# One run of products per piece of the paged cache: scores of piece u beside values of piece u-1

## The chip, the cores and the metric

The kernel runs on one core of a Trainium2 chip. The metric is the device time of one execution in microseconds, as the median over timed runs. The core has a matrix engine (TensorE, PE in the profile; its weight loads are PEld), a vector engine (DVE), a scalar engine (ACT), GpSimd (POOL), a queue engine (SP), and 16 DMA engines that all queues share.

## What is computed

One decoder layer for a prompt group of 512 tokens and a sample group of 8 sequences with 8 tokens each. The 576 tokens are normed and pass one input projection (1024 to 5632 columns). Its columns feed a differential attention (4 heads, two softmax maps each), a gated linear recurrence (4 heads) and two gates. The branches are merged, projected and added to the residual; then come a mixture of 16 experts (two per token), a per-layer input and a last norm.

The change is in the attention of the sample group alone. Its 8 sequences each look at 4096 earlier tokens, which lie in 32 pages of 128 tokens in a paged cache of keys and values. Cut to that part, the reference says:

```python
def page_step(carry, pages):                    # carry: maximum, sum, weighted values
    kp = cache_k[layer, pages]
    vp = cache_v[layer, pages]
    s = jnp.einsum('bthcd,bshcd->bhcts', q, kp).astype(jnp.float32) * scale
    return _online_softmax_update(carry, s, vp), None
carry, _ = lax.scan(page_step, (m0, l0, a0), page_table.T)
```

So for each sequence, head, map and token: scores against all cached keys, their softmax, and the weights times the cached values. All of it is kept in 32-bit floats.

## The kernel before

The kernel's Python builds the whole program ahead of time. Each strand of the work is a "lane", a generator that issues instructions and yields where it needs an event, a free buffer, or nothing but a turn. `run_lanes` picks at each step, among the lanes that can go on and whose estimated time has been reached, the one with the lowest priority number. The estimates come from cost functions (`_cost_pe` and others, and 350 GB/s plus 2 us for a DMA); a DMA's event carries its estimated landing. They count nothing for a change between kinds of product (`SWITCH = 0.0`). The order in which the lanes issue is the order in which each engine runs; on the chip the engines wait only for semaphores, and TensorE goes through its products in that order.

The paged cache is worked off in 32 pieces: a piece u is 8 pages of one sequence, four pieces to a sequence. A piece has four gathers of keys and four of values. Each gather is an indirect DMA of 128 rows of 4 KB (512 KB), issued from GpSimd by `lane_kv`. The order there is four gathers of keys first, then keys and values in turn, so that the keys are always four gathers (one piece) ahead of the values. The buffers are few: NK = 3 tiles for keys that hold two gathers each, and NV = 5 for values that hold one each. GpSimd takes its issues in order, so a gather that waits for a free buffer holds up those behind it.

`lane_scores` makes a piece's scores in two halves, each as soon as its two gathers of keys are in (`kev`), then takes the maximum (DVE), the exponentials (ACT), turns the weights round with four transposes (TensorE) and copies them to `ptz` (two of them); event `ptev[u]`. `lane_values` waits for `ptev[u]`, and for each of the piece's four gathers of values (`vev`) before the products with it. Between the second and the third it yields a turn:

```python
                if j % VW == VW - 1:
                    self.free("V")
                if j == 1:
                    yield
```

Both kinds of product use 32 columns of stationary operand, four heads side by side in the array (`128*32` in the profile). As 32-bit products they show as two instructions each: 32 instructions with 256 moving columns for the scores of a piece, 64 with 128 columns for its values. Most other products use all 128 columns (`128*128`), those of the input projection (`in<-H,hi` and `in<-H,lo`, 288 columns) above all. These belong to `lane_main`, which has a higher priority number and so fills what the other lanes leave. Beside them run the prompt's attention, the recurrence and the routing.

`lane_batches` finishes a sequence after its fourth piece. When all of these lanes and the input projection are through, `lane_mid` closes their buffers; the second branch, the output projection and the experts follow.

Of the kernel before, what the change touches and what calls it, by code (L numbers as in the profile page):

```python
# [20 lines left out]
NB = 8  # L21
# [10 lines left out]
EPS = 1e-6  # L32
# [10 lines left out]
def _consts():  # L43
    """Tables that depend on the shapes alone."""
    p = np.arange(128)
# [54 lines left out]
VW = 1  # L100
# [38 lines left out]
# the weights' chunks in the order of their use  # L139
# [17 lines left out]
def _horder():  # L157
    """The halves of the experts' weights in the order of their use: an expert's second product runs beside the next one's first."""
    r = []
    for tl in range(NE + 2):  # L160
        k, b = wkey(tl), wkey(tl - 1)
        now = [(*k, q) for q in range(4)] if tl <= NE else []
        then = [(*b, q) for q in (4, 5)] if tl else []
        r += now[:2] + then[:1] + now[2:] + then[1:]
    return r + [("pg", k) for k in range(8)]
# [19 lines left out]
class Engine:  # L185
    """Passes instructions on and keeps an estimate of the engine's clock, by which the lanes are interleaved."""
# [62 lines left out]
class Kern:  # L249
# [16 lines left out]
    # ------------------------------------------------ lanes  # L266
# [39 lines left out]
    def pick(self, *tags, n=1):  # L306
        """Which of several tags has n slots free: one that ends in o is for the further tiles until they are through."""
        def f():
            for t in tags:
                if (t[-1] == "o" if self.inner else t[-1] != "o" or self.fev.t is not None):  # L310
                    if self.used.get(t, 0) + n <= self.cap.get(t, 0) - (0 if self.gapev.t is None else self.mres if t == "mr" else self.hres if t == "H" else 0):
                        return t
            return None
        return f
# [12 lines left out]
    def pool(self, st, name, tags, **kw):  # L327
        """A pool with a number of slots per tag, counted as the lanes take and free them."""
# [26 lines left out]
    def aside(self, f):  # L355
        """Runs f without making the lane wait for what it issues; returns the time it ends."""
# [9 lines left out]
    def rstd(self, ss, n, shape):  # L366
        """(ss / n + EPS) ** -0.5 by Newton's steps from the exponent's estimate."""
# [23 lines left out]
    # ---------------------------------------------------------------- start  # L391
# [19 lines left out]
    def setup_rest(self):  # L411
        nc, a = self.nc, self.a
        # lambda, on every partition
# [12 lines left out]
        # 1 for the first map's rows, -lambda for the second's  # L426
# [5 lines left out]
        # lower bound of the forget gate: f = fa + fb * tanh(z / 2)  # L432
# [22 lines left out]
    def lane_start(self):  # L455
        """x * g_mix in two parts, and the norm's factor per token along the free dimension."""
# [87 lines left out]
    # ---------------------------------------------------------------- input projection  # L544
    def issue_w(self, j):
        """Half j % 2 of chunk j // 2 of the weights."""
# [38 lines left out]
    def in_proj(self, i):  # L585
        """One tile of 128 columns of the input projection, for all tokens, with the norm's factor."""
# [68 lines left out]
    def lane_gates(self):  # L655
        """The branches' gates, back from memory."""
# [12 lines left out]
    def to_tok(self, z, tok, tail):  # L669
        """[128, 576] to the token-major [128, 4, 128] and [64, 128]."""  # L670
# [11 lines left out]
    def rope(self, x, c0, c1, sh):  # L682
        """Rotates x ([128, ...] with the positions c0..c1 last) in place."""
# [58 lines left out]
    def lane_attn(self):  # L742
        """Scores and weights of the prompt's attention, by head and block of queries."""
# [38 lines left out]
    def lane_mid(self, waits, st):  # L782
        """When the first phase's lanes are through, their space goes to the next phase's inputs."""
# [13 lines left out]
    # ------------------------------------------------ sample: the new tokens  # L797
# [35 lines left out]
    # ------------------------------------------------ sample: the paged cache  # L833
# [18 lines left out]
    def lane_scores(self):  # L852
        """Scores of 8 pages at a time by (head, page of a pair, token, map), their maxima, weights and sums."""
# [7 lines left out]
        nc.gpsimd.memset(self.xm, 0.0)  # L861
        yield self.qev
        self.query(0)
        for u in range(4 * NB):
            b, q = u // 4, u % 4
            if q == 0 and b > 2:
                yield self.finev[b - 3]
            if q == 2 and b + 1 < NB:
                self.query(b + 1)
            qbd = self.qbd[b].rearrange("p x a n -> p x (a n)")  # L870
            yield ("sc", 1)
            sc = self.tl("sc", [128, 4, 128])
            for j in range(2):
                yield self.kev[4 * u + 2 * j + 1]
                ks = self.ks[2 * u + j].rearrange("p j (d h n) -> p d h j n", d=2, h=4)
                for dh in range(2):
                    for h in range(4):
                        nc.tensor.matmul(sc[32 * h:32 * h + 32, 2 * j:2 * j + 2], qbd[:, h * 2 + dh], ks[:, dh, h], start=dh == 0, stop=dh == 1)
                self.free("K")
# [19 lines left out]
            self.set(self.ptev[u])  # L899

    def lane_values(self):
        nc = self.nc
        acc = self.tl("acc", [128, 4, 128])
        nc.raw.vector.memset(acc, 0.0)
        self.ob = []
        for u in range(4 * NB):
            b, q = u // 4, u % 4
            yield self.ptev[u]
            pt = self.ptz[u % 2].rearrange("p v y h a n -> p v y h (a n)")
            for j in range(4):  # L910
                yield self.vev[4 * u + j]
                vs = self.vs_[(4 * u + j) // VW][:, j % VW].rearrange("p (y h e) -> p y h e", y=2, h=4)
                for y in range(2):
                    for h in range(4):
                        nc.tensor.matmul(acc[32 * h:32 * h + 32, q], pt[:, j % 2, 2 * y + j // 2, h], vs[:, y, h],
                                         start=j == 0 and y == 0, stop=j == 3 and y == 1)
                if j % VW == VW - 1:
                    self.free("V")
                if j == 1:
                    yield  # L920
            self.used["pt"] -= 1
            if q == 3:
                yield ("ob", 1)
                ob = self.tl("ob", [128, 4, 128])
                nc.scalar.copy(ob, acc)
                self.ob.append(ob)
                self.set(self.accev[b])
        self.free("acc")
# [76 lines left out]
    # ------------------------------------------------ prompt attention  # L1005

    # ------------------------------------------------ gated linear recurrence
# [10 lines left out]
    # ---------------------------------------------------------------- branches, output projection  # L1018
# [57 lines left out]
    def rows_setup(self):  # L1076
        """Constants and weights of the routing."""
# [31 lines left out]
    def lane_route(self, i):  # L1109
        """The router's logits of a tile of tokens; its rows with the norm's weights, and behind them what belongs to the norm itself."""  # L1110
# [56 lines left out]
    # ---------------------------------------------------------------- routing  # L1167
# [3 lines left out]
    # ---------------------------------------------------------------- experts  # L1171
# [16 lines left out]
    def lane_msplit(self, keys):  # L1188
        """The first tiles' weights, while the routing is under way."""
# [4 lines left out]
    def lane_mx(self, tiles):  # L1194
        """The tokens' rows of each tile."""
# [26 lines left out]
    # ---------------------------------------------------------------- per-layer input, end  # L1222


    # ---------------------------------------------------------------- all of it
    def run(self):
# [21 lines left out]
        with ExitStack() as ctx:  # L1248
# [18 lines left out]
                     (self.lane_wsplit(), 0), (self.lane_zero(), 0), (self.lane_scores(), 1), (self.lane_values(), 1),  # L1267
# [22 lines left out]
    def more(self, n, who=None):  # L1290
        """A wait for n slots of F beyond those that the other lanes are sure of."""
        return ("F", lambda: n + sum(v for k, v in self.sure.items() if k != who))

    def lane_pv(self):
        """Weights times values, and each head's norm."""
# [49 lines left out]
    def lane_hprep(self):  # L1345
        """Gates, decays and the token-major parts of each head of the recurrence."""
# [51 lines left out]
    def lane_hblocks(self):  # L1398
        """The recurrence's chunks, its norm and its gate."""
        nc = self.nc  # L1400
        for h in range(4):
# [44 lines left out]
            # the sample group: one chunk of 8 per sequence, from its state  # L1446
# [35 lines left out]
            # norm over v, output gate  # L1482
# [36 lines left out]
    def lane_dispatch(self):  # L1519
        """Each token's two experts; token of each slot of each tile, row of each token's two results, experts of the further tiles."""  # L1520
# [129 lines left out]
        # the two weights: softmax over the pair, times the group's probability  # L1650
# [17 lines left out]
    def mload(self, key):  # L1668
        """A half of one part of the experts' weights, 512 KB."""
# [18 lines left out]
    def lane_tail(self, moe):  # L1688
        """Adds each token's experts, then the per-layer input behind its gate and the last norm, tile after tile."""
# [88 lines left out]
        def mixed(gens, rest):  # L1778
            """Steps of chains of small operations, with larger ones between them."""
# [44 lines left out]
    def further(self):  # L1824
        """Tiles beyond the first further one, where the data calls for them."""
# [14 lines left out]
    def query(self, b):  # L1840
        """A batch's queries, apart by page and map: column (page, token, map) of each head and half."""
# [7 lines left out]
    def lane_zero(self):  # L1849
        """The rows of further tiles that stay unused hold zeros."""  # L1850
# [362 lines left out]
```

## Time and profile before

| what | us | share of the span |
|---|---|---|
| median of 3 timed runs (1030.49 to 1032.61) | 1030.66 | |
| span of the profiled execution, first to last instruction | 1028.9 | |
| TensorE busy with products | 957.8 | 93% |
| TensorE's weight loads, beside them | 766.8 | 75% |
| DVE busy | 675.4 | 66% |
| ACT busy | 433.4 | 42% |
| POOL busy | 344.0 | 33% |
| products `sc<-K,qbd` (scores of the cache), 1024 instructions | 68.9 | |
| products `acc<-V,ptz` (values of the cache), 2048 instructions | 80.8 | |

The span is the profiled execution's own time without what lies around its first and last instruction; the timed runs include that. Busy time of TensorE is no measure of how full it is, since its products overlap; the distance between starts is what one more product costs. All records of the program carry the line of one helper (L209), so the groups are told apart by the tiles that they write and read.

### The profile page before, as it was taken

The numbers are of one execution on the slowest core, as the hardware profiler recorded it, in microseconds if no ns is written. First come the engines' busy times: TensorE is split into PE (matmuls) and PEld (weight loads), VectorE is DVE, ScalarE is ACT, GpSimd is POOL, SyncE is SP. The second block draws the span as 40 slices with busy tenths as digits, with TensorE's granted clock in tenths as the row PEclk, the third lists the DMA queues.
The fourth block names the chain that finished last, engine by engine and source line by source line (L and its number), as shares of the span: only waits on it lengthen the run. The fifth ranks groups of instructions, "written<-read, shape, count | busy, mean of one in ns | idle before, by whom it ended". The sixth has DMA issues, their size and how long they took to land. (4 is left out here: it accounts for less than half of the span.)

```text
span 1028.9 us, 20982 instructions
## 1 busy us (share of the span) xinstructions
PE 957.8 (93%) x8129; PEld 766.8 (75%) x8129; DVE 675.4 (66%) x1701; ACT 433.4 (42%) x875; POOL 344.0 (33%) x370
## 2 busy tenths in 40 slices
PE   6999999999999999999999989989639999998995
PEld 5986787877877878778878879868427777775683
DVE  6554555567866774864764465433778999996775
ACT  5143544353342323123222232232228888886442
POOL 3125545454455453543463111332340110101200
PEclk9999999999999999999999989999869999998998
DMA  7549989998989898897997437854149999993511
GB/s 235 206 154 406 367 304 341 313 299 287 335 306 344 311 333 284 297 348 240 332 342 289 139 106 264 291 195 179 46 158 326 393 413 411 412 413 136 186 42 51
DMA packets 93066, 278.67 MB, mean 271 GB/s; under 512 B 10288, under 2 KB 15168, under 8 KB 92960
## 3 DMA queue, kind: packets, MB, share of 16 engines
q0 software_dynamic: 42880, 155.28, 42.5%
q1 hardware_dynamic: 48496, 118.73, 31.7%
q10 hardware_dynamic: 1584, 3.24, 0.8%
q8 instruction: 67, 1.10, 0.4%
q14 instruction: 39, 0.32, 0.1%
HBM read 251.95 MB, written 25.27 MB: 269 GB/s over the span
## 5 line engine op out<-in xcount | busy, mean ns | idle before, releaser
L209 PE MATMUL in<-H,hi 128*128 128x288 f32 x1592 | 357.0, 315 | 14.1 <-ACT hi L209 5.9
L209 PEld LDWEIGHTS in<-H,hi 128*128 128x128 f32 x1592 | 258.9, 193 | 52.1 <-issue 31.3
L209 PE MATMUL in<-H,lo 128*128 128x288 f32 x796 | 239.1, 300 | 0.5 <-DVE lo L209 0.5
L209 POOL DMA_INDIRECT V<-in_vc,idxv x128 | 127.8, 998 | 192.1 <-PE acc L209 172.7
L209 POOL DMA_INDIRECT K<-in_kc,idxk x128 | 126.4, 987 | 104.9 <-PE sc L209 58.1
L209 PEld LDWEIGHTS in<-H,lo 128*128 128x128 f32 x796 | 153.2, 193 | 1.5 <-DVE lo L209 1.2
L209 PE MATMUL in<-mw,xs 128*128 128x512 f32 (+1 forms) x462 | 119.3, 405 | 0.0
L209 DVE TENSOR_TENSOR lo<-raw,hi 128x512 fp32r<-128x512 f32 x116 | 79.7, 691 | 49.5 <-ACT hi L209 48.2
L209 ACT CAST hi<-raw 128x512 fp32r<-128x512 f32 x116 | 70.1, 616 | 84.8 <-PE in L209 58.7
L209 PEld LDWEIGHTS in<-mw,xs 128*128 128x128 f32 (+1 forms) x462 | 85.3, 190 | 20.2 <-DVE xs L209 0.3
L209 PE MATMUL acc<-V,ptz 128*32 128x128 f32 x2048 | 80.8, 277 | 2.1 <-DMA V<-in_vc,idxv 2.0
L209 ACT COPY F<-aux 128x512 f32<-128x512 f32 (+3 forms) x74 | 30.0, 405 | 115.5 <-PE aux L209 115.4
L209 DVE TENSOR_TENSOR mw<-mr,mw 128x1024 fp32r<-128x1024 f32 x58 | 69.2, 1220 | 3.4 <-ACT mw L209 3.4
L209 PEld LDWEIGHTS acc<-V,ptz 128*32 128x32 f32 x2048 | 51.8, 109 | 24.0 <-issue 16.0
L209 PE MATMUL sc<-K,qbd 128*32 128x256 f32 x1024 | 68.9, 387 | 0.7 <-DMA K<-in_kc,idxk 0.7
L209 ACT CAST mw<-mr 128x1024 fp32r<-128x1024 f32 x63 | 65.0, 1056 | 9.0 <-DMA hf_d<-F 7.1
L209 POOL DMA_INDIRECT X<-hf_d,slots x16 | 15.4, 964 | 109.7 <-DVE mw L209 106.0
L209 PE MATMUL aux<-F,F 128*128 128x128 f32 (+6 forms) x216 | 48.0, 394 | 0.2 <-ACT F L209 0.2
L209 DVE TENSOR_TENSOR F<-in,rb 128x288 f32<-128x288 f32 x62 | 27.9, 451 | 29.7 <-PE in L209 29.5
L209 PEld LDWEIGHTS sc<-K,qbd 128*32 128x32 f32 x1024 | 28.3, 110 | 24.0 <-issue 9.3
L209 ACT ACTIVATE F<-F 128x576 f32<-128x576 f32 (+1 forms) x33 | 22.4, 680 | 51.1 <-POOL F L209 26.4
L209 PE MATMUL aux<-mw,hs 128*128 128x512 f32 x150 | 41.8, 415 | 0.5 <-ACT hs L209 0.5
(399 smaller groups left out, 1549.6 us busy)
## 6 DMA issues: line engine op xcount, KB each, us to landing
mr<-in_w_gu SPq DMA_DIRECT2D x55, 512.0 KB, 8.6
raw<-in_w_in SPq DMA_DIRECT2D x88, 256.0 KB, 5.0
mr<-in_w_dn SPq DMA_DIRECT2D x22, 512.0 KB, 10.4
y_d<-Yo SPq DMA_DIRECT2D x17, 512.0 KB, 11.4
raw<-in_w_br SPq DMA_DIRECT2D x16, 256.0 KB, 2.9
raw<-in_w_out SPq DMA_DIRECT2D x16, 256.0 KB, 5.8
H<-in_w_gu SPq DMA_DIRECT2D x7, 512.0 KB, 8.7
y_d<-G SPq DMA_DIRECT2D x1, 3584.0 KB
```

What stands on the lines that cost most here:

```text
L209: return f(*a, **kw)
```

## The change

The lane of the values is gone. The lane of the scores goes through 33 turns instead of 32 pieces. In turn u it waits for everything that the turn needs: the last gather of keys of piece u, the last gather of values of piece u-1, and the weights of piece u-1 (before: each half of the scores waited for its own two gathers, each quarter of the values for its own). Then it issues the scores of u and the values of u-1 with no yield between them, and frees the buffers. The first turn has scores alone, the last one values alone. The rest of a piece (maximum, exponentials, transposes, copies), the buffers, the gathers and their order are as before. Besides, comments and docstrings are gone.

```diff
-        for u in range(4 * NB):
+        for u in range(4 * NB + 1):
             b, q = u // 4, u % 4
+            new = u < 4 * NB
+            if new:
...
+                yield ("sc", 1)
+                sc = self.tl("sc", [128, 4, 128])
+                yield self.kev[4 * u + 3]
+            if u:
+                yield self.vev[4 * u - 1]
+                yield self.ptev[u - 1]
+                if u % 4 == 0:
+                    yield ("ob", 1)
+            if new:
...
+                for j in range(2):
+                    ks = self.ks[2 * u + j].rearrange("p j (d h n) -> p d h j n", d=2, h=4)
+                    for dh in range(2):
+                        for h in range(4):
+                            nc.tensor.matmul(sc[32 * h:32 * h + 32, 2 * j:2 * j + 2], qbd[:, h * 2 + dh], ks[:, dh, h], start=dh == 0, stop=dh == 1)
+                    self.free("K")
+            if u:
+                self.aside(lambda: self.values(u - 1, acc))
+            if not new:
+                break
             yield
...
-    def lane_values(self):
+    def values(self, u, acc):
...
-            for j in range(4):
-                yield self.vev[4 * u + j]
...
-                if j == 1:
-                    yield
...
-                     (self.lane_wsplit(), 0), (self.lane_zero(), 0), (self.lane_scores(), 1), (self.lane_values(), 1),
+                     (self.lane_wsplit(), 0), (self.lane_zero(), 0), (self.lane_scores(), 1), 
```

The body of `values` is the loop of the old lane without its yields: four gathers, for each eight products, then `free("V")`; after a sequence's fourth piece the copy of `acc` to `ob`.

## Rows read from the trace of the kernel before

**Rows 1.** Windows by stage: length, busy time (instructions) per engine, PEclk, DMA share, GB/s
```profile
67.00:588.00 521.00, 513.26 (x5827) 407.14 (x5829) 320.00 (x950) 174.96 (x454) 251.59 (x258) 1.00 0.88 311
588.00:625.00 37.00, 33.67 (x233) 30.82 (x226) 24.03 (x71) 13.06 (x30) 3.76 (x7) 0.86 0.38 110
625.00:763.00 138.00, 111.60 (x632) 90.12 (x630) 74.14 (x213) 36.31 (x70) 44.06 (x36) 0.93 0.54 190
763.00:925.00 162.00, 153.29 (x725) 121.87 (x726) 147.15 (x172) 135.55 (x187) 19.76 (x33) 0.98 0.99 385
```

**Rows 2.** Waits: who waited for whom, us in total, times, longest
```profile
POOL V L209 <- PE acc L209: 172.7, 80, 8.2
...
POOL K L209 <- PE sc L209: 58.1, 23, 28.8
...
PE acc L209 <- DMA V<-in_vc,idxv: 2.0, 1, 2.0
...
PE sc L209 <- DMA K<-in_kc,idxk: 0.7, 1, 0.7
```

**Rows 3.** Timeline of TensorE, a quarter of values, half of scores: start, length, instruction
```profile
572.56 0.43 PE L209 MATMUL in<-H,hi 128*128 128x288 f32 x2
...
573.05 0.65 PE L209 MATMUL acc<-V,ptz 128*32 128x128 f32 x16
573.62 0.54 PE L209 MATMUL in<-H,hi 128*128 128x288 f32 x2
...
574.13 0.43 PE L209 MATMUL in<-H,hi 128*128 128x288 f32 x2
...
574.53 0.43 PE L209 MATMUL in<-H,hi 128*128 128x288 f32 x2
...
575.01 1.07 PE L209 MATMUL sc<-K,qbd 128*32 128x256 f32 x16
576.01 0.53 PE L209 MATMUL in<-H,hi 128*128 128x288 f32 x2
...
576.52 0.43 PE L209 MATMUL in<-H,hi 128*128 128x288 f32 x2
```

**Rows 4.** Timeline of TensorE, a stretch that holds both kinds
```profile
512.43 0.43 PE L209 MATMUL in<-H,hi 128*128 128x288 f32 x2
...
512.92 1.07 PE L209 MATMUL sc<-K,qbd 128*32 128x256 f32 x16
513.80 1.06 PE L209 MATMUL acc<-V,ptz 128*32 128x128 f32 x32
514.79 0.54 PE L209 MATMUL in<-H,hi 128*128 128x288 f32 x2
...
515.30 0.43 PE L209 MATMUL in<-H,hi 128*128 128x288 f32 x2
```

**Rows 5.** Timeline of TensorE, the cache's first and last stretch of products
```profile
67.14 1.93 PE L209 MATMUL sc<-K,qbd 128*32 128x256 f32 x32
...
587.84 0.65 PE L209 MATMUL acc<-V,ptz 128*32 128x128 f32 x16
```

**Rows 6.** Timelines of TensorE and POOL where gathers follow freed buffers
```profile
482.45 0.64 PE L209 MATMUL acc<-V,ptz 128*32 128x128 f32 x16
...
483.40 0.93 POOL L209 DMA_INDIRECT V<-in_vc,idxv  x1 [8.22 <-PE acc L209]
484.64 0.94 POOL L209 DMA_INDIRECT K<-in_kc,idxk  x1 [0.30 <-PE acc L209]
...
488.37 0.94 POOL L209 DMA_INDIRECT V<-in_vc,idxv  x1 [0.30 <-issue]
```

**Rows 7.** Instructions on tile V: from a gather's issue to its landing
```profile
DMA to landing us min/median/max: 4.0/6.7/9.7
```

**Rows 8.** Timeline of TensorE and ACT, from the last values to the sample's attention output
```profile
588.55 0.58 ACT L209 COPY ob<-acc 128x512 f32<-128x512 f32 x1 [0.51 <-PE acc L209]
...
608.36 0.30 PE L209 MATMUL aux<-constb,yo 128*128 128x128 f32 x1
```

More of the change, by code (lines that the diff above doesn't have):

```diff
@@ L861, in lane_scores @@
         nc.gpsimd.memset(self.xm, 0.0)
+        acc = self.tl("acc", [128, 4, 128])
+        nc.raw.vector.memset(acc, 0.0)
+        self.ob = []
         yield self.qev
         self.query(0)
-        for u in range(4 * NB):
+        for u in range(4 * NB + 1):
             b, q = u // 4, u % 4
[L866 to L879, printed above, removed]
+            new = u < 4 * NB
+            if new:
+                if q == 0 and b > 2:
+                    yield self.finev[b - 3]
+                if q == 2 and b + 1 < NB:
+                    self.query(b + 1)
+                yield ("sc", 1)
[7 more added lines that the diff above has]
+            if new:
+                qbd = self.qbd[b].rearrange("p x a n -> p x (a n)")
+                for j in range(2):
[8 more added lines that the diff above has]
+                break
             yield
@@ L899, in lane_scores @@
             self.set(self.ptev[u])
-    def lane_values(self):
+        self.free("acc")
+    def values(self, u, acc):
         nc = self.nc
[L903 to L909, printed above, removed]
-            for j in range(4):
-                yield self.vev[4 * u + j]
[L912 to L918, printed above, removed]
-                if j == 1:
-                    yield
[L921 to L928, printed above, removed]
+        b, q = u // 4, u % 4
+        pt = self.ptz[u % 2].rearrange("p v y h a n -> p v y h (a n)")
+        for j in range(4):
+            vs = self.vs_[(4 * u + j) // VW][:, j % VW].rearrange("p (y h e) -> p y h e", y=2, h=4)
+            for y in range(2):
+                for h in range(4):
+                    nc.tensor.matmul(acc[32 * h:32 * h + 32, q], pt[:, j % 2, 2 * y + j // 2, h], vs[:, y, h],
+                                     start=j == 0 and y == 0, stop=j == 3 and y == 1)
+            if j % VW == VW - 1:
+                self.free("V")
+        self.used["pt"] -= 1
+        if q == 3:
+            ob = self.tl("ob", [128, 4, 128])
+            nc.scalar.copy(ob, acc)
+            self.ob.append(ob)
+            self.set(self.accev[b])
     def lane_batches(self):
```

## The prediction

> **What bounds the kernel now.** I read the windows by stage first. From 67 to 588 us, where the cache is worked off, TensorE is busy for 513.26 of 521 us at the full granted clock, while DVE has 320 and POOL 252; the DMA engines stand at a share of 0.88 and 311 GB/s [rows 1]. The reader is to see an engine with no holes and a DMA that is heavily used but not full: in the experts' stage the same share reads 0.99 at 385 GB/s. Second come the waits, to see which of the two, TensorE or DMA, is behind the other. GpSimd's gathers wait for buffers that TensorE frees, 172.7 us for values and 58.1 for keys; TensorE waits for gathers 2.0 and 0.7 us [rows 2]. So the gathers run ahead, and TensorE's order sets the end of this stage. Third, the timeline of TensorE tells what a stretch of the cache's products costs.
>
> After 588 us nothing hangs on absolute time: the stage behind it is fed by products of the first, and in 625 to 763 the DMA share is 0.54, which leaves room for the experts' weights that are fetched early there [rows 1]. What the first stage gains, the end gains.
>
> **The price of a stretch.** Two starts of the `hi` pair of the input projection lie 0.40 us apart where nothing comes between (574.13 to 574.53). Over a quarter of values it is 572.56 to 574.13 for two such turns, so 1.57 - 0.80 = 0.77 us for 16 instructions; over half the scores 574.53 to 576.52, 1.99 - 0.80 = 1.19 us [rows 3]. A stretch that holds half the scores and two quarters of values costs 512.43 to 515.30, 2.87 - 0.80 = 2.07 us [rows 4]. Apart these three would be 1.19 + 2 x 0.77 = 2.73. The difference, 0.66 us, is two changes into the 32-column products and out again: **0.33 us for each stretch**, whatever its length. What is left is 0.86 us for half the scores and 0.44 for a quarter of values.
>
> The part of the rows that shows it: the first `hi` pair behind a stretch lasts 0.53 to 0.54 instead of 0.43 us, and its next one starts 0.51 later instead of 0.40 [rows 3]. The Trainium skill (TensorEngine Tiling (Array Packing), Key Properties) says that changing the tiling mode drains the engine, while different tiles of one mode run side by side. Of a drain it states some 128 cycles (TensorE: Matmul & The Clock Gate, Part 2), an estimate of 0.053 us at 2.4 GHz or 0.11 for the way in and out; by that the 98 stretches counted below would give 10 us and not 32. The measured 0.33 decides, the way back costs more than a drain.
>
> **What goes.** Between the first and the last stretch [rows 5] I count 147 stretches of 32-column products with the cache in them, 131 of the cache alone and 16 in which other lanes' 32-column products stand too. The change makes 33, and the 16 others may then stand alone: 49 in place of 147, so 98 x 0.33 = 32.3 us less. In some 35 of the 147 one neighbour is another tiled product (64 rows or 64 columns), with a change of its own that stays; for their share of the removed ones, 98/147 x 35 = 23, I take half the price off, 23 x 0.17 = 4. **About 28 us of TensorE go.** Products, softmax, copies and gathers are the same in number. The loop has the same yields behind the scores, and the wait for `ob` only moves ahead of the fourth piece's values. These cost nothing beside a full TensorE.
>
> **What is added** is one wait for everything. Before, a quarter of values ran and freed its buffer while others loaded. Now five buffers of values and three tiles of keys turn over once per piece. Four of the values and two tiles of keys are taken by the turn itself; what can load ahead of it is one gather of values and one tile of keys. Five more gathers (values, keys, values, keys, values) must follow the turn's own first freed buffer of values, since GpSimd issues in order and the next gather in line is of values.
>
> The shortest distance from turn to turn then follows. The scores of a turn take 2 x 0.86 = 1.72 us. From the start of a quarter of values to the issue of the gather that it frees it is 482.45 to 483.40, 0.95 us; the five issues then take 483.40 to 488.37, 4.97 us [rows 6]; the last lands 6.7 us later at the median [rows 7]. Sum: 1.72 + 0.95 + 4.97 + 6.7 = **14.3 us**, with 11.6 at the fastest landing (4.0) and 17.3 at the slowest (9.7).
>
> TensorE's own distance: the 32 pieces take 67.14 to 587.84 [rows 5], 521/32 = 16.3 us each; less 28/32 = 0.9 it is **15.4 us**. On the mean the gathers keep 1.1 us ahead. But both scatter. TensorE is in order: behind a turn that waits stands the whole input projection, so a late gather costs its full lateness, and an early one gives nothing back. The bounds of this cost are zero (every turn's gathers at 14.3 or below, or the lanes' order spaced to them) and 32 x (17.3 - 15.4) = 61 us (each at the slowest landing). I take 8 us, a quarter of a microsecond per turn: nearer to zero, because the median landing lies under TensorE's distance and because the lanes' order puts a turn no earlier than its estimated landings. The DMA's mean rate has to rise by 521/501 to some 323 GB/s, under the 385 of the experts' stage [rows 1].
>
> For a gather of 512 KB the Trainium skill (DMA: Bandwidth & Descriptors, Anatomy of one DMA) gives 2.0 us and the bytes at 436 GB/s, an estimate of 3.2 us; by that a turn could follow after 10.8 us, nothing would wait, and the change would give the whole 28. The landing of 6.7 us, taken among other transfers, speaks against counting on it.
>
> **The sum.** 1028.9 - 28 + 8 = 1009 us of span. The median of the timed runs lies 1.8 us above the span, which I leave as it is: **1010.5 us**. The tail behind the last values (588.55 to 608.36 until the sample's output is turned [rows 8]) stays; TensorE has the first branch's products beside it (33.67 of 37 us busy [rows 1]).
>
> **The rivals.**
> *Nothing waits.* The gathers stay ahead as before; for it speaks that GpSimd was held up for 172.7 us by full buffers [rows 2], against it that these waits were of a buffer at a time. 1030.7 - 28 = 1003, down to 998 if the 16 shared stretches also merge.
> *The gathers become the bound* (the other side). Bursts of five gathers behind each turn queue behind the weights, and landing takes 9 us in place of 6.7: 16.6 us a turn, 32 x (16.6 - 15.4) = 38 us of holes in TensorE, 1030.7 - 28 + 38 = 1041. It decides from a landing of 7.6 us on (the distance is then TensorE's 15.4) and costs more than the change brings from 8.5 on. For it: the slowest landing is 9.7 [rows 7], and the DMA share is 0.88 already. Against it: a weight of the input projection that is served later holds nothing up as long as it is buffered.
> *The gain is given back at the end of the stage.* The turns come in an order set by estimates that know neither the 0.33 nor GpSimd's 1.24 us per issue. If by them the cache falls some pieces behind the input projection, the last of them run with nothing beside them: one trailing turn leaves 14.3 - 3.8 (its products: 1.72 + 4 x 0.44 + 0.33) = 10.5 us of TensorE idle, and two of them 21, of which the first branch's products hide part. 1030.7 - 28 + 8 + 10 to 20 = 1021 to 1031. For it: the last stretch stands at 587.84 among the last products of the input projection, with no reserve of such work behind it.
> *It doesn't do what it says*, and the products still fall into many stretches: there is no yield within a turn, so I give it no chance of its own.
>
> **How the numbers follow.** Forecast (1004 to 1017) 0.44; nothing waits (996 to 1004) 0.15; given back (1017 to 1031) 0.22; gathers as the bound (1031 and up, mostly to 1045) 0.19. A measurement of this kernel can tell 0.2%, 2 us, from no change. Faster by that: 0.44 + 0.15 and most of the third, 0.78; within it 0.05; slower 0.17. The range goes from 998 to 1036: it leaves some 0.05 below and 0.14 above.
>
> **What would show it.** The timeline of the changed kernel has 33 stretches with the cache in them, of 32 scores and 64 values, some 3.8 us from start to start of the next `hi` pair. The waits of TensorE for `V` and `K`, 2.7 us before, stand near 8 to 10; above 30 the second rival is right, near 3 the first. The landing of `V` stays by 6.7. The last values lie near 568 with input-projection products up to them; if TensorE has holes between turns behind the last `in<-H` product of the input projection, it is the third. The prediction is wrong if the stretches fall as said and TensorE is nevertheless no sooner through the stage for another reason than gathers, or if a stretch's 0.33 us turns out to belong to something that stays.

## The result and the profile after

The changed kernel takes 1035.98 us (median of 14 runs, 1030.37 to 1039.37), the kernel before 1025.59 beside it (14 runs, 1023.2 to 1033.36): a ratio of 1.0077, 95% interval 1.0054 to 1.0099. It is slower by 0.8%. Forecast were 1010.5 us, 2% faster; the range reached to 1036. The profiled execution of the changed kernel took 1030.37 us, with a span of 1028.6, as long as the span of 1028.9 of before.

That execution is the shortest of the 14. So the two traces show where the gain went, but not the 10 us that lie between the medians. What is on record beside these is the mean granted clock of each run: 0.964 at the median of the changed kernel's 14 (0.969 in a run of 1031 us, 0.961 in two of 1038 and 1039), and 0.972 to 0.973 for the kernel before, beside e1 to e4 and e13 to e18. That the clock makes the difference is not shown: e3 below ran at 0.962 and took 1028.5 us.

Windows by stage, after, the columns as in [rows 1]:
```profile
67.00:588.00 521.00, 495.03 (x5846) 422.77 (x5848) 320.99 (x955) 176.98 (x458) 249.43 (x258) 0.99 0.86 311
588.00:625.00 37.00, 34.44 (x264) 31.69 (x257) 24.00 (x72) 12.63 (x29) 3.73 (x7) 0.91 0.37 117
625.00:763.00 138.00, 111.88 (x576) 87.70 (x574) 66.12 (x192) 34.94 (x66) 44.47 (x36) 0.89 0.51 182
763.00:925.00 162.00, 149.30 (x718) 118.80 (x719) 146.45 (x184) 132.04 (x185) 19.70 (x33) 0.97 0.97 379
```
From 67 to 588 us TensorE is busy 18.2 us less than in [rows 1]. The cache takes as long as before: the last values product starts at 588.7 (588.2 before), the input projection's last product at 586.8 (593.9). From 67 us to the end of both kinds TensorE is busy 496.0 us after (to 588.9) and 519.5 before (to 594.2). It does this work in 23.5 us less, near the 28 forecast; it is through 5 us sooner and stands idle for the other 18.

The timeline of TensorE, after, around one turn (answers to [rows 3, 4]):
```profile
125.23 0.53 PE L209 MATMUL in<-H,hi 128*128 128x288 f32 x2
125.60 0.30 PE L209 MATMUL in<-H,lo 128*128 128x288 f32 x1
125.82 1.93 PE L209 MATMUL sc<-K,qbd 128*32 128x256 f32 x32
127.57 1.93 PE L209 MATMUL acc<-V,ptz 128*32 128x128 f32 x64
129.43 0.53 PE L209 MATMUL in<-H,hi 128*128 128x288 f32 x2
```
The 33 stretches are there, 3.61 us from the scores' start to the next product. What TensorE waits for instead, from the views of waits: first the five longest rows of after (100 to 590 us), then the two longest of before in the same window.
```profile
PE aux L209 <- ACT F L209: 7.0, 7, 1.6
PE in L209 <- DVE F L209: 6.0, 4, 2.4
PE sc L209 <- DMA K<-in_kc,idxk: 3.6, 1, 3.6
PE aux L209 <- DVE F L209: 2.3, 2, 2.1
PE aux L209 <- DVE pnT L209: 2.2, 1, 2.2
```
```profile
PE in L209 <- DVE F L209: 1.9, 2, 1.0
PE sc L209 <- ACT P L209: 1.5, 4, 0.6
```
Gathers have one wait of 3.6 us for keys in it, and no more. GpSimd still stands before full buffers, now once per turn, from its view of waits and the instructions on tile `V`, after (answers to [rows 2, 7]):
```profile
POOL V L209 <- PE acc L209: 200.6, 31, 11.5
```
```profile
DMA to landing us min/median/max: 4.0/6.2/10.0
```
The other waits are for VectorE's and ScalarE's results. All gaps of 150 ns and more in front of TensorE's products from 100 to 590 us, summed from the trace, are 23.8 us after (20.2 without the wait for keys) and 4.5 before; "gaps" below always means this sum. One of them, timelines of TensorE and then VectorE, after:
```profile
254.85 0.53 PE L209 MATMUL in<-H,hi 128*128 128x288 f32 x2
255.22 0.29 PE L209 MATMUL in<-H,lo 128*128 128x288 f32 x1
257.46 0.58 PE L209 MATMUL in<-H,hi 128*128 128x288 f32 x1 [1.94 <-DVE F L209]
```
```profile
253.94 0.58 DVE L209 TENSOR_SCALAR F<-F,fc 128x576 f32<-128x576 f32 x1
...
255.00 1.36 DVE L209 TENSOR_TENSOR_SCAN F<-F,d 128x576 f32<-128x576 f32 x1
256.27 0.67 DVE L209 TENSOR_TENSOR lo<-raw,hi 128x512 fp32r<-128x512 f32 x1
256.86 0.45 DVE L209 TENSOR_TENSOR F<-in,rb 128x288 f32<-128x288 f32 x1
```
TensorE needs a PSUM buffer that `F<-in,rb` reads out. VectorE gets to it at 256.86, behind a scan and a weight's split that stand ahead of it in its own order. Not all are of this kind: of the seven waits in `PE aux L209 <- ACT F` above, five (6.0 us) are for a ScalarE that had itself been idle for 1.6 to 2.3 us, until VectorE gave it a row statistic. At three of the five longest waits TensorE's granted clock falls, at 234, 257 and 275 us, to 0.50 for some 3.4 us each. Windows of 225 to 300 us, after; before, all three read 1.00:
```profile
225.00:250.00 25.00, 22.59 (x314) 20.18 (x304) 13.60 (x54) 9.16 (x28) 12.44 (x14) 0.93 0.83 314
250.00:275.00 25.00, 20.64 (x212) 17.92 (x211) 15.96 (x49) 4.94 (x12) 10.51 (x11) 0.92 0.75 266
275.00:300.00 25.00, 24.82 (x314) 20.64 (x313) 16.41 (x53) 7.48 (x18) 11.66 (x12) 0.94 0.85 310
```
ScalarE too stands at the turns, from its view of waits after; before, these two rows were 22.4 us in 11 waits and 7.2 in 4:
```profile
ACT P L209 <- DVE sm L209: 75.9, 20, 9.0
...
ACT ob L209 <- PE acc L209: 34.4, 6, 8.9
```

The 7 us by which the input projection ends sooner are lost further on, where the first branch's products meet the output projection's. The waits of TensorE from 625 to 680 us, before and then after:
```profile
PE acc L209 <- ACT hi L209: 0.8, 1, 0.8
```
```profile
PE acc L209 <- ACT hi L209: 7.4, 3, 4.9
```
The window of 640 to 655 us, before and then after:
```profile
640.00:655.00 15.00, 14.64 (x87) 12.68 (x87) 8.00 (x15) 4.29 (x8) 3.44 (x3) 1.00 0.78 273
```
```profile
640.00:655.00 15.00, 13.97 (x67) 11.98 (x68) 4.17 (x7) 2.79 (x6) 1.41 (x1) 0.78 0.79 282
```
The timeline of ScalarE and TensorE, after, at the wait of 4.86 us:
```profile
639.70 0.68 ACT L209 ACTIVATE F<-F 128x576 fp32r<-128x576 f32 x1 [3.03 <-POOL F L209]
640.29 1.64 ACT L209 CAST hi<-raw 128x512 fp32r<-128x512 f32 x3
...
640.94 0.80 PE L209 MATMUL acc<-hi,F 128*128 128x512 f32 x1 [4.86 <-ACT hi L209]
```
The cast of the weight stands on ScalarE behind a merged row's step, and those rows come through VectorE and GpSimd one in 3.7 us. TensorE came 6.2 us sooner to this place (the last product of the branch's twelfth block starts at 635.8 instead of 642.0) and left it and a like one behind: its sixteenth is there at 671.8, before 666.4. Of these 11.6 us, 6.6 are waits (7.4 less 0.8); the window shown has a granted clock of 0.78 instead of 1.00. The experts' first product starts at 771.3, before 766.9. From there to the end it is 257.3 us, before 262.0, so that the spans come out level; the clock differs there too, in 925 to 1029 us, before and then after:
```profile
925.00:1029.00 104.00, 88.23 (x363) 62.91 (x361) 70.14 (x190) 45.28 (x88) 10.62 (x11) 0.92 0.31 106
```
```profile
925.00:1029.00 104.00, 87.73 (x379) 62.89 (x377) 73.41 (x193) 48.74 (x92) 10.56 (x11) 0.97 0.35 123
```

### The profile page after: what moved, and what is told of

Same layout as the page of the kernel before. It is cut to its first block, busy times and chain, and to the rows that moved or that the text cites. A ratio compares the mean times of both kernels' runs of the same rounds, so it can differ in the third digit from the quotient of the medians.

```text
span 1028.6 us, 20889 instructions
## 1 busy us (share of the span) xinstructions
PE 935.5 (91%) x8129; PEld 776.9 (76%) x8129; DVE 670.8 (65%) x1701; ACT 433.1 (42%) x875; POOL 342.3 (33%) x370
## 5 line engine op out<-in xcount | busy, mean ns | idle before, releaser
L209 PE MATMUL in<-H,hi 128*128 128x288 f32 x1600 | 352.9, 313 | 17.6 <-DVE F L209 7.0
L209 PEld LDWEIGHTS in<-H,hi 128*128 128x128 f32 x1600 | 263.9, 194 | 38.1 <-issue 14.5
L209 PE MATMUL in<-H,lo 128*128 128x288 f32 x800 | 241.1, 301 | 0.0
L209 POOL DMA_INDIRECT V<-in_vc,idxv x128 | 125.0, 976 | 230.2 <-PE acc L209 200.6
L209 PEld LDWEIGHTS in<-H,lo 128*128 128x128 f32 x800 | 154.8, 194 | 0.3 <-DVE lo L209 0.3
L209 POOL DMA_INDIRECT K<-in_kc,idxk x128 | 127.2, 994 | 82.0 <-issue 37.2
L209 PE MATMUL in<-mw,xs 128*128 128x512 f32 (+1 forms) x462 | 117.0, 399 | 0.0
L209 DVE TENSOR_TENSOR lo<-raw,hi 128x512 fp32r<-128x512 f32 x116 | 79.4, 692 | 57.5 <-ACT hi L209 56.3
L209 ACT CAST hi<-raw 128x512 fp32r<-128x512 f32 x116 | 69.4, 617 | 81.0 <-PE in L209 39.1
L209 PEld LDWEIGHTS in<-mw,xs 128*128 128x128 f32 (+1 forms) x462 | 83.7, 186 | 19.4 <-DVE xs L209 0.3
L209 DVE TENSOR_TENSOR mw<-mr,mw 128x1024 fp32r<-128x1024 f32 x58 | 69.3, 1221 | 3.0 <-ACT mw L209 3.0
L209 ACT CAST mw<-mr 128x1024 fp32r<-128x1024 f32 x63 | 65.0, 1056 | 9.5 <-DMA hf_d<-F 8.1
L209 PE MATMUL sc<-K,qbd 128*32 128x256 f32 x1024 | 62.5, 383 | 3.6 <-DMA K<-in_kc,idxk 3.6
L209 PE MATMUL acc<-V,ptz 128*32 128x128 f32 x2048 | 62.0, 273 | 0.0
L209 ACT COPY F<-aux 128x128 f32<-128x128 f32 (+3 forms) x74 | 29.8, 405 | 75.6 <-PE aux L209 75.3
L209 PEld LDWEIGHTS acc<-V,ptz 128*32 128x32 f32 x2048 | 57.4, 110 | 5.3 <-issue 0.2
L209 ACT ACTIVATE P<-sc,sm 128x512 f32<-128x512 f32 x32 | 22.0, 688 | 75.9 <-DVE sm L209 75.9
L209 POOL DMA_INDIRECT X<-hf_d,slots x16 | 15.3, 958 | 107.2 <-DVE mw L209 97.1
L209 PEld LDWEIGHTS sc<-K,qbd 128*32 128x32 f32 x1024 | 30.1, 110 | 25.6 <-issue 8.4
L209 PE MATMUL aux<-F,F 128*128 128x128 f32 (+6 forms) x216 | 47.3, 387 | 0.9 <-ACT F L209 0.9
L209 ACT ACTIVATE F<-F 128x576 f32<-128x576 f32 (+1 forms) x33 | 22.3, 679 | 50.5 <-POOL F L209 36.0
L209 DVE TENSOR_REDUCE stm<-sc 128x1 f32<-128x512 f32 x32 | 22.0, 688 | 30.6 <-PE sc L209 30.6
```

The source lines that it names most:

```text
L209: return f(*a, **kw)
```

## The experiments

Ratios are to the kernel before, timed beside it on the same chip. The runs fell on five chips, of two kinds. On the first kind (three chips) the kernel before takes 1028 to 1029 us (e1 to e4, e13 to e18), on the second (two chips) 1070 to 1071 (e5 to e12). Theory A: the waits belong to the newly drawn order (the planner writes another order for any change, and that of before is a good one). Theory B: the removed switches had covered VectorE's and ScalarE's chains. Theories C and D, in the texts on e13 to e16, are about the second kind of chip: C has the bursts of gathers stop the engines there, D the written order. The texts on the first four runs number the theories as they stood then.

**e1, e2: the planner's constant HOP 0.5 instead of 0.2, on after and on before.**
```
-HOP, HOP2, DLAT = 0.2, 0.2, 2.0
+HOP, HOP2, DLAT = 0.5, 0.2, 2.0
```


> The changed kernel, with the planner's estimate of the way from one engine to another raised from 0.2 to 0.5 us; the instructions are the same, only their order is planned anew. Theory 1 (lost cover): the time that the changes between kinds of product took stood in no estimate and kept TensorE behind ACT and DVE; without it TensorE comes to products whose inputs are not ready, 24.8 us of waits between 100 and 592 us against 4.5 before. Then longer estimated ways space the chains, the waits in that stretch fall below 12 us and the input projection ends by 577 us or earlier (586.8 in the changed kernel). Theory 2 (the turn itself): the waits come from the unbroken turn of 3.8 us and what stands right behind it; then longer ways alter little, 20 us or more of waits stay. Theory 3 (order by chance): the order of the whole stage is re-drawn with every edit and the waits scatter, with no direction.

> The kernel before with the same longer ways (0.5 us) in the planner. Theory 1: TensorE had no waits to lose there (4.5 us between 100 and 592), so the end of the input projection stays within 4 us of 593.9 and the whole within 5 us of the kernel before. Theory 3: the order is drawn anew and the stage's end moves by as much as it did with the change, 5 to 10 us, either way.


After: 1034.31 us, 1.0041 (1.0016 to 1.0067), gaps 27.5 us. Before: 1055.6 us, 1.0279 (1.0227 to 1.0332), gaps 23.5 us. Longer planned hops take no wait away. But the kernel before, newly drawn, has 23.5 us of gaps too. It has 107 stretches in this order, not 147, so this run alone does not part a new order from fewer switches. With the same constant on both sides the change is worth 1055.6 - 1034.3 = 21 us; 74 stretches less at 0.33 us would be 24.

**e3: the values' time counted to the lane, so that the softmax is planned behind them.**
```
-                self.aside(lambda: self.values(u - 1, acc))
+                self.values(u - 1, acc)
```


> The changed kernel, but the lane's estimated time goes on over the values of the turn (they are no longer issued aside), so that the maximum, the exponentials and the four transposes of the piece are planned 2.1 us later. Theory 2: the waits of the transposes right behind a turn (13 of 33 turns, 0.2 to 1.1 us each) go, with the blocked ACT and DVE behind them; the stage gains 5 us or more. Theory 1: only these 3 to 4 us go, and the other waits (17 us or more) stay.


1028.47 us, 1.0007 (0.9985 to 1.003), gaps 23.4 us. The fastest version of the change that ran, level with before. Its gaps are those of after, so the softmax's planned place is not their cause.

**e4: the kernel before with a yield behind each quarter of values.**
```
-                if j == 1:
+                if j < 3:
```


> The kernel before with a turn yielded behind each of the four gathers of values instead of behind the second alone, so that the values fall into up to 64 more stretches. If a stretch costs its 0.33 us on the path that sets the end (theory 1 and the prediction), 50 to 64 more stretches make the stage 16 to 21 us longer (the input projection ends at 610 to 615 us, the whole is 1.5 to 2% slower). If the price was never on that path (theory 3), the stage's end stays within 6 us.


0.9997 (0.9967 to 1.0027). The planner wrote the same order as before, so this is a second measurement of the kernel before: gaps 4.5 us again.

**e5 to e8: small nudges of the planner, HOP 0.20 to 0.21 or DLAT 2.0 to 2.1, on before and on after.**
```
-HOP, HOP2, DLAT = 0.2, 0.2, 2.0
+HOP, HOP2, DLAT = 0.21, 0.2, 2.0
```
```
-HOP, HOP2, DLAT = 0.2, 0.2, 2.0
+HOP, HOP2, DLAT = 0.2, 0.2, 2.1
```


> The kernel before with one constant of its planner moved by 0.01 us (HOP 0.20 to 0.21), nothing else: the same instructions in another order. Theory A (the order of the kernel before is a rare good one; any new order brings TensorE waits on ScalarE's and VectorE's results, 20 to 28 us between 100 and 590 us against 4.5): 1.01 to 1.04 of the time before, TensorE's gaps of 150 ns and more between 100 and 590 us together 15 us or more, the input projection ends after 598 us. Theory B (the switches in and out of 32-column products had covered ScalarE's and VectorE's chains, so that waits come only with fewer switches): within 0.5% of the time before, gaps 8 us or less, with 140 or more stretches.

> The kernel after with the same constant moved by 0.01 us. Theory A: a new draw of the changed kernel's order, its waits of 100 to 590 us again 18 to 28 us, the time within 1.5% of the kernel after on either side, below the same re-draw of the kernel before by 15 us or more. Theory B: the waits are 20 to 28 us too, and the time lies at or above the re-drawn kernel before.

> The kernel before with the planner's DMA latency moved from 2.0 to 2.1 us. Theory A: 1.01 to 1.04 of the time before, gaps of TensorE from 100 to 590 us 15 us or more. Theory B: within 0.5%, gaps 8 us or less.

> The kernel after with the planner's DMA latency moved from 2.0 to 2.1 us. Theory A: below the kernel before with the same constant by 15 us or more, gaps 18 to 28 us. Theory B: at or above it, gaps 20 to 28 us.


Before: 1.0269 (1.0211 to 1.0327) and 1.0007 (0.9973 to 1.004). After: 1.1976 (1.1931 to 1.2021) and 1.1932 (1.1878 to 1.1986). Neither theory has a place for 1.19. The gaps of e5 and e7 are 38.7 and 22.3 us, but there is no trace of the unchanged kernel before from this kind of chip to hold them against, so neither theory could be judged there.

**e9 to e12: the kernel after unchanged, the HOP 0.21 orders again, and before with VectorE's planned fixed cost 0.072 instead of 0.070.**
```
-    return 0.07 + n * (0.00104 if name != "reciprocal" else 0.0063)
+    return 0.072 + n * (0.00104 if name != "reciprocal" else 0.0063)
```


> The kernel after, unchanged, beside its and the old kernel's re-drawn orders on one chip. On the chip of e5 to e8 the re-drawn changed kernels took 1.19 to 1.20 of the time before, with 6 to 8 us from a turn's last values product to the copy of its sums (0.34 us in all other runs). If that is the chip (turns with all their gathers in front of them meet late landings there), the kernel after takes 1.15 to 1.2 there too and 1.005 to 1.01 on a chip like the first; if it is the order, it stays at 1.005 to 1.01 anywhere.

> The kernel after with HOP 0.21, the order of e6. If the order made it slow: 1.19 again. If the chip did: 0.99 to 1.015 on another chip, with TensorE's waits of 100 to 590 us at 18 to 28 us.

> The kernel before with HOP 0.21, the order of e5, which took 1.027. Theory A (the order of the kernel before is a good draw): 1.015 to 1.035 on another chip too, waits of 15 us or more between 100 and 590 us. If e5 was the chip's: within 0.5% and 8 us or less.

> The kernel before with the planner's fixed cost of a VectorE instruction 0.072 us instead of 0.070, nothing else. Theory A: 1.01 to 1.04, waits of 15 us or more. Theory B (the switches covered the other engines' chains): within 0.5%, waits of 8 us or less.


After unchanged: 1270.24 us, **1.1855** (1.1811 to 1.1899); e10 1.1973 (1.193 to 1.2017), e11 1.0309 (1.0268 to 1.0349), e12 1.0027 (0.9993 to 1.0061). So it goes with the chip, and it meets the change: in each of three orders the changed kernel takes 19 to 20% more on this kind of chip. No two sets of these runs share a chip, so a lasting property of the chip and its condition at that time are not told apart. Windows behind one turn whose last values product starts at 110.9 us in e9 (the first fence), and at 114.1 in after on the first kind (the second):
```profile
111.00:115.00 4.00, 3.54 (x31) 2.35 (x20) 0.00 (x0) 0.52 (x2) 2.99 (x4) 1.00 0.82 251
115.00:119.00 4.00, 2.15 (x13) 1.56 (x11) 0.00 (x0) 0.02 (x1) 1.88 (x2) 0.97 1.01 395
119.00:123.00 4.00, 1.65 (x6) 1.30 (x7) 2.26 (x7) 2.21 (x7) 1.87 (x2) 0.50 0.92 330
123.00:127.00 4.00, 4.00 (x18) 4.00 (x19) 2.24 (x6) 0.94 (x4) 0.00 (x0) 0.50 0.58 202
```
```profile
114.00:118.00 4.00, 3.70 (x42) 3.27 (x33) 3.08 (x7) 1.92 (x6) 3.08 (x4) 1.00 0.87 247
118.00:122.00 4.00, 4.00 (x33) 3.89 (x32) 2.87 (x9) 2.70 (x6) 3.08 (x4) 1.00 1.02 359
122.00:126.00 4.00, 4.00 (x35) 3.53 (x37) 0.98 (x2) 3.18 (x9) 1.27 (x2) 1.00 0.99 363
```
In both, eight gathers follow a turn and the DMA engines are full (0.9 to 1.0). On the first kind all engines work on. In e9 VectorE and ScalarE stand while the burst lasts and TensorE more and more; behind the burst TensorE, which was busy 2.15 and 1.65 of 4 us, runs on at a granted clock of 0.50, the lower of its two levels (1.2 GHz). Over 27 turns TensorE is idle 36 to 73% of the time from 2 to 10 us behind a turn (in stretches of 2 us), and 6% or less from 12 us on, some 150 us in all; in after it was some 20. What waits for TensorE's products starts late there as well, timelines of TensorE and ScalarE in e9:
```profile
548.36 1.93 PE L209 MATMUL acc<-V,ptz 128*32 128x128 f32 x64
...
557.98 0.58 ACT L209 COPY ob<-acc 128x512 f32<-128x512 f32 x1 [14.59 <-remote]
```
The copy starts 8.0 us after the last start of these products, and ScalarE stands idle ahead of it; in after and in before it was 0.34 to 0.35 us in most batches (the text on e9 says in all).

**e13, e14: light gathers.** Each gather that fills a buffer again brings 64 of a row's 1024 columns, on after and on before, with the order of every engine unchanged.
```
+   out=at[:, :c], in_=self.a[src] if c == 1024 else self.a[src].rearrange("r (a c) -> (r a) c", c=64),
```


> The kernel after in its own order, but each gather that fills a buffer again brings 64 of a row's 1024 columns (the products then read old data in the rest); number, order and waits of the gathers stay. Theory C (eight gathers right behind a turn fill the DMA engines, and on some chips every engine then stands): where e9 took 1.19, this takes 0.93 to 0.97 of the full kernel before, TensorE's idle time from 70 us to the last values falls from 176 us to under 30; on a chip like the first, 0.97 to 0.99. Theory D (the written order makes ScalarE and VectorE wait, whatever DMA does): 1.1 or more where e9 took 1.19, and on a chip like the first 1.00 to 1.01 with 18 to 26 us of TensorE's gaps from 100 to 590 us.

> The kernel before with the same light gathers. Theory C: where e5 to e12 ran (full kernel before 1070) it loses the 40 us that it takes more there, 0.955 to 0.975; on a chip like the first 0.99 to 1.00. The light after lies under it by the switches' 20 to 30 us. Theory D: the light after lies level with it or above.


They fell on a chip of the first kind: 1033.07 us, 1.0055 (1.0025 to 1.0084), and 1025.12, 0.9953 (0.9927 to 0.9978). First stage of e13, then e14:
```profile
67.00:588.00 521.00, 496.60 (x5851) 424.49 (x5854) 321.85 (x955) 177.15 (x458) 251.33 (x258) 0.99 0.25 82
```
```profile
67.00:588.00 521.00, 515.47 (x5860) 409.96 (x5859) 322.49 (x961) 176.47 (x457) 254.51 (x258) 1.00 0.25 81
```
With the DMA share at 0.25 instead of 0.86 the gaps are 22.6 us (4.5 in e14), and TensorE's row is that of after. On this kind of chip the bytes of the gathers have no part in the loss: the text of theory D holds here, and that of theory C (0.97 to 0.99 for e13, and below e14) does not. What they do on the second kind these runs don't tell.

**e15: a yield between a turn's scores and its values. e16: six small memsets of GpSimd in front of each gather into a used buffer.**
```
             if u:
+                yield
                 self.aside(lambda: self.values(u - 1, acc))
```
```
+            if j >= 6:
+                for _ in range(6):
+                    nc.raw.gpsimd.memset(self.pace, 0.0)
```


> The kernel after with a yield between the scores and the values of a turn, so that other lanes' products may stand between: two bursts of four gathers instead of one of eight, and 65 stretches instead of 33. Theory C: where e9 took 1.19, 1.03 to 1.12; on a chip like the first 0.99 to 1.01. Theory D: 1.17 or more, since the order's waits stay.

> The kernel after with six small GpSimd memsets (together some 0.7 us) in front of each gather that fills a buffer again: eight gathers in some 16 us instead of 10. Theory C: where e9 took 1.19, less, 1.08 to 1.16, though the last gather of a turn is issued later; on a chip like the first slower, 1.02 to 1.06, since turns then wait for gathers. A plain bound by the gathers' landing would be 1.22 or more where e9 took 1.19.


e15: 1.0057 (1.0029 to 1.0085), with 33 stretches as before the edit: the planner put nothing between, so it tells nothing of bursts. It is one more order of the changed kernel, with gaps of 28.1 us. e16: 1.1063 (1.1004 to 1.1121), slower than either text gave, and 32 pieces that take from 67 to 691.5 us, 19.5 each. From its view of waits:
```profile
PE sc L209 <- DMA K<-in_kc,idxk: 76.4, 21, 9.2
...
POOL V L209 <- PE acc L209: 10.5, 16, 2.0
```
TensorE now waits for gathers, but GpSimd hardly waits for buffers (200.6 us in after). Its gathers follow each other at 2.51 us on the mean from 100 to 650 us, so the eight of a piece take 20 us, about as long as a piece. The bound of e16 is thus GpSimd's own rate with the memsets in it. How much the turns of after have to spare it does not tell.

**e17: the switches put back into after. e18: the order of e12 again.** In e17 every engine's order is that of after, but between the scores' groups of 8 stand extra products of one column on 128 columns of weights, 96 in all; their sums are overwritten.
```
+                        if (j, dh) != (1, 1):
+                            nc.raw.tensor.matmul(acc[:, (u - 1) % 4, 0:1], ident, ident[:, 0:1], start=True, stop=True)
```


> The kernel after with the order of every engine unchanged, but in each of its 32 runs of scores three extra products of one column on 128 columns of weights stand between the groups of 8, their sums overwritten later: 96 more stretches of 32-column products, near the 98 that the change took away. By rows of the kernel after (0.20 us out, 0.22 us in, 0.09 us saved) each adds some 0.33 to 0.4 us, 32 to 38 us of TensorE. Theory B (the switches were cover for ScalarE's and VectorE's chains, so that a freed us comes back as a wait): most of it vanishes, the time rises by 8 to 18 us over the kernel after and the gaps of 100 to 590 us fall from 24 to under 10 us. Theory A (the gaps are of the written order, switch or no switch): it rises by 30 to 40 us and the gaps stay at 18 to 26 us. On a chip like that of e9 the rise is read against 1.186.

> The kernel before with VectorE's fixed cost in the planner 0.072 instead of 0.070, the order of e12, now for a chip like the first. Theory A (4.5 us of gaps is a rare good draw): gaps of 100 to 590 us 15 us or more and 1.010 to 1.03 of the time before. Theory B: within 0.5%, gaps 8 us or less. On a chip like that of e9 it is 1.00 again and tells nothing new.


e17: 1068.01 us, 1.0398 (1.0365 to 1.0431), against 1.0077 for after: 3.2% or 33 us more. Its timeline of TensorE:
```profile
97.61 0.64 PE L209 MATMUL sc<-K,qbd 128*32 128x256 f32 x8
98.18 0.38 PE L893 MATMUL acc<-constb 128*128 128x1 f32 x2
98.49 0.64 PE L209 MATMUL sc<-K,qbd 128*32 128x256 f32 x8
```
The input projection's last product starts at 623.6 us (586.8 in after), so each extra stretch costs 36.8 / 96 = 0.38 us, the product of one column included. Gaps from 100 to 632 us, the longer stage, are 21.5, hardly fewer (15.2 to 590 us). Theory B as its text puts it falls: TensorE's time given back shows in full at the end of the stage, and the waits stay nearly as long. But these switches stand inside the turns. Whether the removed ones were cover where they stood, between the other lanes' products, no run tests.

e18, before with another order on a chip of the first kind: 1041.58 us, 1.0108 (1.006 to 1.0156), with 156 stretches and the input projection's last product at 606.8 (593.9). Its gaps are 7.3 us. So not every new order brings waits of 15 us or more: theory A falls in that form. The time (1.0108) is not that of theory B's text either (within 0.5%). What holds is that an order nobody meant to change moves the kernel by up to 3%: 1.0108 in e18 and 1.0279 in e2 on the first kind, on the second 1.0007 (e7), 1.0027 (e12) and 1.027 to 1.031 (e5, e11). Nine stretches at 0.38 are 3 us of e18's 13 in the stage; where the others are was not followed up.

On the first kind of chip there are then four orders of the changed kernel, two of them with a small edit beside (1.0007 in e3, 1.0041 in e1, 1.0057 in e15, 1.0077), and three of the kernel before (1, 1.0108 in e18, 1.0279 in e2). With so few, what the change is worth apart from the draw is not shown.

## Why the prediction was wrong

*The price of a stretch, 0.33 us, and 28 us in all*: right in the main. After has 23.5 us less TensorE work up to the end of the cache and the input projection, and e17 gives 0.38 us per stretch with its extra product. By the drain of some 128 cycles that the Trainium skill names (TensorE: Matmul & The Clock Gate, Part 2) e17's 96 ways out and in would have cost an estimated 10 us; they cost 36.8, the extra products included.

*The shortest distance by gathers, 14.3 us, and 8 us of waits for them*: the term was too large. TensorE waited 3.6 us for one gather; gathers of values landed after 6.2 us at the median. By the prediction's own sign ("near 3 the first") that is the rival "nothing waits": it had the gathers right and the time (996 to 1004) wrong. The margin of 1.1 us itself was not tested, since e16 is bound by GpSimd.

*"TensorE's order sets the end of this stage"*: this held for the kernel before, and was carried over to a kernel with another order. **The step that failed is "These cost nothing beside a full TensorE."** The sum put TensorE's waits for VectorE and ScalarE at nothing. The condition, a full TensorE, went with the change: the planner wrote a new order of all engines, in which TensorE waits 20.2 us for VectorE's and ScalarE's results (23.8 with the one gather), against 4.5. That these waits took most of the gain in the first stage (18 of 23.5 us) is measured. Why the new order has them is argued by exclusion: not the bytes of the gathers (e13), not the softmax's planned place (e3), not the switches' time as such (e17). One rival is left, that the removed switches were cover in the places where they stood: on the first kind of chip the two orders with over 140 stretches have 4.5 and 7.3 us of gaps, the others 21 to 28 (e17 counted to 632 us, and without e16). "What would show it" named the case at its end only: through the stage no sooner, for another reason than gathers.

*"What the first stage gains, the end gains"*: wrong too. The 7 us that did reach the end of the input projection were lost, with 4.4 more, by the experts' first product; 6.6 us of that are waits at places where ScalarE's casts stand behind rows that come at 3.7 us each. In the experts' stage 4.7 us came back, at a higher granted clock than before; the prediction had no term for that either.

The rival "given back at the end of the stage" came near in time (1021 to 1031; the profiled run took 1030, the median is 1036), not in mechanism: there are no trailing turns. "The gathers become the bound" had the side and, on the first kind of chip, not the cause. So it is luck that the time touches the upper end of the range: that end was put there for gathers. Two slips in the working change nothing: 1028.9 - 28 + 8 + 1.8 is 1010.7, and by the same rows landing costs more than the change brings from 8.6 us on, not 8.5.

Open stay: which instruction of the new order makes it wait, since a single edit redraws everything; what makes the typical run 10 us longer while the traces are level; why e18 is slower with few gaps; and what stops the engines on the second kind of chip. There the full DMA burst and the standing of the engines coincide, which is not yet a cause; no run with the bytes taken away fell on such a chip.

## What to carry to other kernels

Where a planner writes the order, an edit of one lane is a new draw for all of them: measure it against several redrawn kernels before as well (here one pair gave 1.004 against 1.028, and the orders as written 1.008 against 1), and expect up to 3% from the draw alone. A freed microsecond of a full engine is a gain only if what feeds it comes sooner too. And a change that turns a steady stream of transfers into bursts should be timed on more than one chip.

## What the runs showed of the hardware

Chips differ for the same program: the kernel before took 1026 to 1031 us on some and 1070 to 1071 on others, the kernel after 1.0077 and 1.1855 of it. On the second kind some 20% of the landings' records were missing from the traces (7,987 left in e8, 10,072 in after), and the time from the start of TensorE's last product of a batch to the copy that waits for it was 5.1 to 8.0 us in six of eight batches of e9, against 0.34 to 0.35 in six of eight of after.

A change out of 32-column products and back costs some 0.33 us of TensorE in place ([rows 3, 4]), 0.38 with a one-column product between (e17).
